# Depthwise convolution by even and odd tokens, conv blocks laid between head pairs, and GpSimd kept for the MLP, in a hybrid RWKV-7 and convolution layer

## The chip, the core and the metric

The kernel runs on one core of a Trainium2 chip. The metric is the time of one execution in device microseconds (us), as the median of several runs. Engines are called PE (TensorE, matrix products), DVE (VectorE), ACT (ScalarE), POOL (GpSimd) and SP (SyncE, which issues transfers). Each runs its own queue of instructions in order; a wait of the first holds up all behind it.

## The reference

One layer of 1024 tokens and 1024 channels, in float32. The input is normalised and projected onto 2816 columns; 1792 go to eight RWKV-7 heads, 1024 to a gated convolution of 512 channels with 31 taps. The results are joined and projected back, and an MLP with a squared ReLU follows.

```python
h = rmsnorm(x, norm_mix_g[l])
p = h @ w_in[l]                                  # 1024 x 2816
p_rwkv = p_rwkv + (token_shift(p_rwkv) - p_rwkv) * shift_mu[l]
y_rwkv = rwkv7_group(p_rwkv, ...)                # 8 heads x 64, state S_t = S_{t-1}(diag(w_t) + a_t b_t^T) + v_t k_t^T
# conformer_conv_group
h = u[..., :D_CONV] * jax.nn.sigmoid(u[..., D_CONV:])
h = lax.conv_general_dilated(h, conv_w[:, None, :], window_strides=(1,),
        padding=[(30, 0)], feature_group_count=512) + conv_b
# ... layer norm over the 512 channels, silu
x = x + jnp.concatenate([y_rwkv, y_conv], axis=-1) @ w_out[l]
h = rmsnorm(x, norm_mlp_g[l])
x = x + jnp.square(jax.nn.relu(h @ w_ff1[l])) @ w_ff2[l]
return rmsnorm(x, norm_final_g)
```

## The kernel before

**Products.** An operand is split into a high and a low part and multiplied in three products (high by high, low by high, high by low). The input projection takes 22 weight blocks of 128 columns: `load_w` fetches a block into `wraw` (one buffer), ACT rounds it to `wh` (L219) and POOL forms `wl`, the rest (L220); there are two buffers of each. A block is multiplied in two halves of 512 tokens, each 48 matmuls of 256 columns (8 slices of channels, three products, two pieces of 256 tokens).

**Convolution.** Channels lie on partitions, in four blocks of 128. `conv_block(cb)` projects a block's two halves (gate and value), writes the gated result `h2` of 30 + 1024 columns (L312), and puts 31 taps into a list: a first one that also adds the bias (L317) and 30 that multiply `h2`, shifted by a token each, by one weight per channel and add it to `acc` (L319), each on all 1024 columns, on DVE. `do_taps(n)` writes out the next n taps.

**RWKV heads.** The heads go in four pairs p of 0 to 3 and two halves of 512 tokens. `decays` makes the decays with a scan (L407); `mix_block` projects r, k and v; `stage1(p, h)` forms what the recurrence needs in chunks of 64 tokens (AR at L425 and L426, kq, KB, AM at L448, a diagonal `dg` at L456 by which KB is multiplied on PE for `kt`); `solve(g)` inverts the triangular systems of a group of two pairs in 30 rounds of two small DVE operations (L505, L507); `merge(g, h)` brings its result through DRAM back to another layout (QT, L524). Then `step(g)` runs one of 16 chunks of a group's recurrence: POOL scales the state (`SP`, L585), PE multiplies, DVE adds the new state (L601).

**After them.** `conv_norm` transposes and normalises the convolution's channels and splits them (`cvl`, L669); `load_wout` splits the output weights (`wol`, L692); `out_first` and `out_second` add output products to the residual (L699), `post` finishes a head group's output (`yo`, L629). The first products of the MLP are mixed in, and the MLP itself follows by half-size blocks.

**Order.** A written-out sequence of calls at the end of the program gives each call its priority; a scheduler places instructions by it and by their dependences, engine by engine. The two lines of `load_w` that split a block are

```python
        S.activation(wh, raw, AF.Copy)
        G.tensor_tensor(wl, raw, wh.bitcast(F32), op=ALU.subtract)
```

where `S` is ACT, `G` POOL and `V` DVE. Every matmul is recorded at L96 and every transpose on PE at L99, inside a helper; there the names of the PSUM banks (ca, cb, ya, yb, ps, pr) tell the work apart.

Of the kernel before, what the change touches and what calls it, by code (L numbers as in the profile page):

```python
# [9 lines left out]
F32 = mybir.dt.float32  # L10
# [21 lines left out]
CUT = (2, 2)  # L32
H2B = 2
DIRECT = 4
# [18 lines left out]
def hymba_layer(ctx: ExitStack, tc: tile.TileContext, a: dict, out: bass.AP):  # L53
# [242 lines left out]

    accs = [None] * 4
    taps = []
    gate = {"solve": None}

    def conv_block(cb):
        tag = in_banks[-1]
        wg, wu = load_w(CG + cb * P), load_w(CU + cb * P)
        h2 = hc.tile([P, TAPS - 1 + T], F32, name="h2", bufs=H2B)
        V.memset(h2[:, 0:TAPS - 1], 0.0)
# [7 lines left out]
        accs[cb] = cv.tile([P, T], F32, name="acc", bufs=4)  # L313

        def tap(j):
            if j == 0:
                return V.tensor_scalar(accs[cb], h2[:, 0:T], cw[:, 0, cb:cb + 1], prm("conv_b", cb), op0=ALU.mult, op1=ALU.add)  # L317
            else:
                return V.scalar_tensor_tensor(accs[cb], h2[:, j:j + T], cw[:, j, cb:cb + 1], accs[cb], op0=ALU.mult, op1=ALU.add)  # L319
# [97 lines left out]
    def stage1(p, h):  # L417
# [22 lines left out]
        G.tensor_tensor(KB[:, :, 1, :], c8(kq), c8(Ei), op=ALU.mult)  # L440
        for i in range(2):
# [133 lines left out]
    def chain(g, c, yb):  # L575
        e = c % 2
        L1, KB, rhs, Arb, Th = tiles.pop((g, c))
        b = bank("ca" if g == 0 else "cb")
        lo = b.t[0:64, 0:256].rearrange("p (n t) -> p n t", n=4)
        hi = b.t[0:64, 256:512].rearrange("p (n t) -> p n t", n=4)  # L580
        yr = yb.t[64 * e:64 * e + 64, 0:256].rearrange("p (n t) -> p n t", n=4)
        SR = cp.tile([P, 4, C], F32, name="SR", bufs=2)
        SP, R = SR[0:C], SR[C:P]
        if c < 15:
            G.tensor_tensor(SP, rhs[0:64], PC[:, c, 4 * g:4 * g + 4, None].to_broadcast([C, 4, C]), op=ALU.mult)  # L585
        hops = []
        for n in range(4):
            i = b.mm(lo[:, n, :], L1[:, n, 0:C], rhs[:, n, :], True, True)
        hops.append(i)
        S.copy(R, lo)  # L590
        for n in range(4):
            yb.mm(yr[:, n, :], L1[:, n, C:P], rhs[:, n, :], n == 0, False)
        for n in range(4):
            i = b.mm(lo[:, n, :], Th[:, n, :], R[:, n, :], True, True)
        hops.append(i)
        S.copy(rhs[0:64], lo)
        if c < 15:
            for n in range(4):
                i = b.mm(hi[:, n, :], KB[:, n, :], rhs[:, n, :], True, True)
            hops.append(i)  # L600
            V.tensor_tensor(tiles[g, c + 1][2][0:64], hi, SP, op=ALU.add)  # L601
        for n in range(4):
            yb.mm(yr[:, n, :], Arb[:, n, :], rhs[0:64, n, :], False, n == 3)
        if g == 1:
            pace.update(hops=hops, n=0)

    def post(pool, d):
# [19 lines left out]
        for p in range(NP):  # L627
            S.activation(yo[:, p, :], b.t[:, p * P:(p + 1) * P], AF.Identity, scale=prm("ln_x_g", p), bias=prm("ln_x_b", p))
        G.tensor_tensor(yo, yo, bon, op=ALU.add)  # L629
        V.tensor_tensor(yo, yo, bg.t.rearrange("p (n t) -> p n t", n=NP), op=ALU.mult)  # L630
# [6 lines left out]
    def conv_norm(ln, ct, h):  # L637
        yc = [ln.tile([P, 512], F32, name=f"yc{t}") for t in range(4)]
        mv = ln.tile([P, 4, 2], F32, name="mv")
        for t in range(4):  # L640
            b = bank()
            for cb in range(4):
                b.tr(b.t[:, cb * P:(cb + 1) * P], accs[cb][:, (4 * h + t) * P:(4 * h + t + 1) * P], ident)
# [13 lines left out]
        for cb in range(4):  # L657
# [26 lines left out]
    def load_wout(pool, raws, ks):  # L684
        for n in range(2):
            for k in ks:
# [288 lines left out]
    stage1(1, 1)  # L975
    do_taps(4)
    do_taps(4)
    do_taps(4)
    do_taps(4)
    do_taps(4)  # L980
    do_taps(4)
    do_taps(4)
    do_taps(4)
    do_taps(4)
    do_taps(4)
    do_taps(4)
    do_taps(4)
    do_taps(2)
# [60 lines left out]
    step(0)  # L1049
    step(0)  # L1050
# [307 lines left out]
```

## Time and profile before

| | us |
|---|---|
| median of 3 runs | 1330.41 |
| lowest and highest run | 1326.93 and 1331.7 |
| the profiled execution, by the same clock as the runs | 1334.43 |
| its span in the trace, first to last instruction | 1332.7 |
| PE busy in it | 1229.8 |
| DVE busy | 960.9 |
| ACT busy | 539.6 |
| POOL busy | 291.1 |

Busy times are sums over instructions, with overlaps counted once. Matmuls overlap in the record, so PE's is no measure of how fast it works. The mean granted clock of PE over the span is .961 of full speed.

### The profile page before, as it was taken

Reading aid. Unit: us, or ns where it says so; the run is one execution under the profiler, and the core shown is the slowest. Engines: PE = TensorE matmul, PEld = TensorE weight load, DVE = VectorE, ACT = ScalarE, POOL = GpSimd, SP = SyncE. Lnnn points to the kernel's source line nnn. Section 1 sums busy time; section 2 is a strip of 40 time slices with the busy share of each in tenths; the row PEclk is TensorE's granted clock in tenths of the full one; section 3 lists DMA queues with packets and bytes.
Section 4 is the critical chain, followed back from the end, with each engine's and each line's share of the span. In section 5 each row is a group of like instructions: output and inputs, shape, how many; then the busy total and the mean of one; then the engine's idle time right before and its main releaser. Section 6 shows DMA issues by size and latency. Waiting matters only on the chain.

```text
span 1332.7 us, 20860 instructions
## 1 busy us (share of the span) xinstructions
PE 1229.8 (92%) x8171; PEld 1059.0 (79%) x8171; DVE 960.9 (72%) x1440; ACT 539.6 (40%) x937; POOL 291.1 (22%) x181
## 2 busy tenths in 40 slices
PE   6999899988998859999999999999948899999996
PEld 5999788887896748899988788888837688888885
DVE  6379965698999672444669766665428898897997
ACT  6313233322323363333468454545533333433345
POOL 2124143332333153311000000000004324231420
PEclk9999899998998778999999999999978899999999
DMA  5211445525626667536135554543157425223003
GB/s 185 56 48 37 109 112 145 132 72 122 155 59 158 160 162 186 176 112 178 44 110 183 159 162 142 163 134 124 66 167 267 142 80 158 63 81 93 16 1 126
DMA packets 194475, 161.44 MB, mean 121 GB/s; under 512 B 54387, under 2 KB 153785, under 8 KB 194377
## 3 DMA queue, kind: packets, MB, share of 16 engines
q1 hardware_dynamic: 181192, 157.90, 40.0%
q10 hardware_dynamic: 13056, 2.13, 0.9%
q8 instruction: 64, 1.05, 0.3%
q14 instruction: 35, 0.28, 0.1%
q0 software_dynamic: 128, 0.08, 0.0%
HBM read 110.23 MB, written 49.84 MB: 120 GB/s over the span
## 4 chain that ended last, share of the span: by engine, by line
PE 60%; DVE 24%; DMA 7%; issue 4%; ACT 2%; SPq 1%; POOL 1%; DVEq 0%; ACTq 0%
PE ps L96 27%; DVE acc L319 9%; PE yb L96 9%; PE ya L96 8%; PE cb L96 7%; PE ca L96 5%; PE pr L96 3%; DMA lk_d<-kt 2%; DVE Q L507 2%; DVE Qt L505 1%; DVE bl L827 1%; DVE sA L1187 1%; DVE al L827 1%; DVE ta L437 1%; PE ps L99 1%
## 5 line engine op out<-in xcount | busy, mean ns | idle before, releaser
L319 DVE SCALAR_TENSOR_TENSOR acc<-h,cw,acc 128x1024 f32<-128x1024 f32 x120 | 176.8, 1493 | 1.1
L826 ACT ACTIVATE ah<-sA 128x1024 fp32r<-128x1024 f32 x32 | 34.0, 1061 | 135.3 <-PE pr L96 50.1
L96 PE MATMUL ps<-bh,ah 128*128 128x512 f32 x168 | 65.7, 404 | 22.4 <-ACT bh L826 16.5
L220 POOL TENSOR_TENSOR wl<-wraw,wh 128x1024 fp32r<-128x1024 f32 x22 | 56.6, 2572 | 136.1 <-ACT wh L219 136.1
L1187 POOL TENSOR_TENSOR sB<-B,B11e 128x1024 f32<-128x1024 f32 x4 | 11.6, 2890 | 337.5 <-DMA B<-in_w_ff_dram 335.2
L96 PE MATMUL cb<-hh,wh 128*128 128x256 f32 x264 | 79.4, 301 | 5.1 <-DVE k L257 3.1
L96 PE MATMUL cb<-hl,wh 128*128 128x256 f32 x264 | 79.9, 302 | 0.1
L96 PE MATMUL cb<-hh,wl 128*128 128x256 f32 x264 | 77.8, 295 | 0.0
L96 PE MATMUL ps<-bl,ah 128*128 128x512 f32 x168 | 68.1, 405 | 4.0 <-DVE bl L827 3.9
L96 PE MATMUL yb<-hh,wl 128*128 128x256 f32 x248 | 71.5, 288 | 0.0
L96 PE MATMUL yb<-hh,wh 128*128 128x256 f32 x248 | 71.4, 288 | 0.0
L96 PE MATMUL yb<-hl,wh 128*128 128x256 f32 x248 | 71.0, 286 | 0.0
L96 PE MATMUL ps<-bh,al 128*128 128x512 f32 x168 | 67.5, 402 | 0.0
L827 DVE TENSOR_TENSOR al<-sA,ah 128x1024 fp32r<-128x1024 f32 x32 | 50.5, 1580 | 23.6 <-ACT ah L826 23.6
L827 DVE TENSOR_TENSOR w1l<-s,w1h 128x512 fp32r<-128x512 f32 x64 | 43.9, 687 | 24.8 <-ACT w1h L826 24.8
L826 ACT ACTIVATE w1h<-s 128x512 fp32r<-128x512 f32 x64 | 40.3, 632 | 50.5 <-PE ps L96 29.0
L96 PEld LDWEIGHTS cb<-hh,wh 128*128 128x128 f32 x264 | 53.2, 202 | 9.0 <-DVE k L257 3.3
L96 PEld LDWEIGHTS cb<-hl,wh 128*128 128x128 f32 x264 | 53.1, 201 | 4.8 <-issue 4.0
L96 PEld LDWEIGHTS ps<-bh,ah 128*128 128x128 f32 x168 | 32.9, 197 | 30.2 <-ACT bh L826 16.9
L585 POOL TENSOR_TENSOR SR<-rhs,PC 64x256 f32<-64x256 f32 x30 | 28.6, 953 | 124.8 <-DVE rhs L601 104.8
L96 PEld LDWEIGHTS cb<-hh,wl 128*128 128x128 f32 x264 | 53.3, 202 | 2.3 <-issue 2.0
L846 ACT ACTIVATE c<-c 128x512 f32<-128x512 f32 x60 | 38.0, 633 | 38.2 <-DVE c L932 21.5
(460 smaller groups left out, 4008.8 us busy)
## 6 DMA issues: line engine op xcount, KB each, us to landing
w1r<-in_w_ff_dram SPq DMA_DIRECT2D x44, 512.0 KB
hid_d<-c SPq DMA_DIRECT2D x64, 256.0 KB
LK<-lk_d SPq DMA_DIRECT2D x32, 384.0 KB
A<-hid_d SPq DMA_DIRECT2D x24, 512.0 KB
B<-in_w_ff_dram SPq DMA_DIRECT2D x24, 512.0 KB
wraw<-in_w_in_dram SPq DMA_DIRECT2D x22, 512.0 KB
xt<-in_x_dram SPq DMA_DIRECT2D x8, 512.0 KB
lk_d<-AR SPq DMA_DIRECT2D x16, 256.0 KB
```

The source lines that it names most:

```text
L96: return self._order(PE.matmul(o, lhsT=lhsT, rhs=rhs, start=start, stop=stop, skip_group_check=more))
L99: self._order(PE.transpose(o, in_, identity))
L220: G.tensor_tensor(wl, raw, wh.bitcast(F32), op=ALU.subtract)
L319: return V.scalar_tensor_tensor(accs[cb], h2[:, j:j + T], cw[:, j, cb:cb + 1], accs[cb], op0=ALU.mult, op1=ALU.add)
L437: V.scalar_tensor_tensor(ta, ta, 1.0, Ei, op0=ALU.add, op1=ALU.mult)
L505: V.tensor_tensor(o, Q[:, 0:s, s:s + 1].to_broadcast([R, s, n]), Q[:, s:s + 1, s + 1:32].to_broadcast([R, s, n]), op=ALU.mult)
L507: V.tensor_tensor(Q[:, 0:s, s + 1:32], Q[:, 0:s, s + 1:32], o, op=ALU.add)
L585: G.tensor_tensor(SP, rhs[0:64], PC[:, c, 4 * g:4 * g + 4, None].to_broadcast([C, 4, C]), op=ALU.mult)
L826: S.activation(hi, src, AF.Copy)
L827: V.tensor_tensor(lo, src, hi.bitcast(F32), op=ALU.subtract)
L846: S.activation(c, c if src is None else src, AF.Relu)
L1187: engine.tensor_tensor(t, x, y, op=op)
```

## The change

Three things are changed together.

First, the convolution works on even and odd tokens. `h2` has three rows of 16 + 512 columns: even tokens, odd tokens and their sums (two sums of 256 columns each at L318 after, behind the two h2 writes at L316). The 16 even taps act on the even tokens (into `acc[:, 0]`), the 15 odd taps on the odd ones (into `odd`), and 16 taps with summed weights (`cws`) on the sums (into `acc[:, 1]`); `join` subtracts the first two from the third for the odd outputs and adds them, one token apart, for the even ones. So 31 operations on 1024 columns become 47 on 512 (three of them first ones, which also add the bias) and 3 joins on 512. `h2` has one buffer where it had two. `conv_norm` reads the halves and writes its results at a stride of two columns.

Second, whatever POOL did ahead of the MLP on large tiles goes to DVE: `wl` (22 times), kq, KB and r in `stage1` (8 each), `SP` (30), `wol` (16), `yo` (8) and `cvl` (8). `dg` and its product are replaced: ACT scales KB by the decay (64 operations of 128x128, into `kd`), and PE transposes that.

Third, the sequence of calls is rewritten: a conv block stands ahead of each head pair, with its taps behind the pair's `stage1`; conv block 3 comes after `stage1(3, 1)`; `solve(1)` and the merges come ahead of `conv_norm`; and steps of group 1 begin between those of group 0.

```diff
-H2B = 2
+H2B = 1
...
-        G.tensor_tensor(wl, raw, wh.bitcast(F32), op=ALU.subtract)
+        V.tensor_tensor(wl, raw, wh.bitcast(F32), op=ALU.subtract)
...
+    cws = const.tile([P, 16, 4], F32, name="cws")
+    V.tensor_copy(cws[:, 0], cw[:, 0])
+    V.tensor_tensor(cws[:, 1:16], cw[:, 1:30:2], cw[:, 2:31:2], op=ALU.add)
+    cb2 = derived("cb2", 4, prm("conv_b", 0, 4), 2.0, None)
...
-        h2 = hc.tile([P, TAPS - 1 + T], F32, name="h2", bufs=H2B)
+        h2 = hc.tile([P, 3, 16 + 512], F32, name="h2", bufs=H2B)
...
-            o = TAPS - 1 + h * 512
-            V.scalar_tensor_tensor(h2[:, o:o + 512], th, 1.0, bu, op0=ALU.add, op1=ALU.mult)
...
+            o = slice(16 + h * 256, 16 + h * 256 + 256)
+            V.scalar_tensor_tensor(h2[:, 0:2, o].rearrange("p e n -> p n e"), th.rearrange("p (n e) -> p n e", e=2), 1.0,
+                                   bu.rearrange("p (n e) -> p n e", e=2), op0=ALU.add, op1=ALU.mult)
+            V.tensor_tensor(h2[:, 2, o], h2[:, 0, o], h2[:, 1, o], op=ALU.add)
...
+            o, c = ((acc[:, 0], cw[:, 2 * i, cb:cb + 1]), (odd[:, 1:513], cw[:, max(2 * i - 1, 0), cb:cb + 1]), (acc[:, 1], cws[:, i, cb:cb + 1]))[ph]
+            x = h2[:, ph, i + 1:i + 1 + 512]
...
+            return V.scalar_tensor_tensor(o, x, c, o, op0=ALU.mult, op1=ALU.add)
...
+        def join(*_):
+            V.tensor_tensor(acc[:, 1], acc[:, 1], acc[:, 0], op=ALU.subtract)
+            V.tensor_tensor(acc[:, 1], acc[:, 1], odd[:, 1:513], op=ALU.subtract)
+            return V.tensor_tensor(acc[:, 0], acc[:, 0], odd[:, 0:512], op=ALU.add)
...
-        G.tensor_tensor(kq, kq, k, op=ALU.mult)
+        V.tensor_tensor(kq, kq, k, op=ALU.mult)
...
-            dg = mp.tile([P, 4, P], F32, name="dg", bufs=1)
-            G.tensor_tensor(dg, ident[:, None, :].to_broadcast([P, 4, P]),
-                            E1[:, 4 * q:4 * q + 4, C:C + 1].to_broadcast([P, 4, P]), op=ALU.mult)
+            kd = mp.tile([P, 4, P], F32, name="kd", bufs=1)
+            for c in range(4):
+                S.activation(kd[:, c, :], KB[:, 4 * q + c].rearrange("p j t -> p (j t)"), AF.Copy, scale=E1[:, 4 * q + c, C:C + 1])
...
-                bk.mm(bk.t[:, c * P:(c + 1) * P], KB[:, 4 * q + c].rearrange("p j t -> p (j t)"), dg[:, c, :], True, True)
+                bk.tr(bk.t[:, c * P:(c + 1) * P], kd[:, c, :], ident)
...
-            G.tensor_tensor(SP, rhs[0:64], PC[:, c, 4 * g:4 * g + 4, None].to_broadcast([C, 4, C]), op=ALU.mult)
+            V.tensor_tensor(SP, rhs[0:64], PC[:, c, 4 * g:4 * g + 4, None].to_broadcast([C, 4, C]), op=ALU.mult)
...
+    step(0)
+    conv_block(3)
     do_taps(8)
-    stage1(3, 1)
-    step(0)
-    step(0)
+    step(0)
+    solve(1, (0, 1))
+    step(0)
+    merge(1, 0)
+    step(0)
+    do_taps(23)
...
-    solve(1, (0, 1))
+    step(0)
     wo = open_pool("wo", side="right")
     load_wout(wo, wo, (4, 5, 6, 7))
-    merge(1, 0)
-    step(0)
-    merge(1, 1)
-    step(0)
-    step(0)
-    step(0)
+    step(0)
+    step(1)
+    step(0)
+    step(1)
```

On DVE, in the first `stage1` of head pair 0, the queue of before alternates taps of the two conv blocks (h_719 is block 0's h2, h_936 block 1's):

```order
L319 SCALAR_TENSOR_TENSOR acc<-h_936,cw,acc 128x1024
L437 SCALAR_TENSOR_TENSOR ta<-ta,Ei 128x512
L319 SCALAR_TENSOR_TENSOR acc<-h_719,cw,acc 128x1024
L337 MEMSET pm 128x1
L425 SCALAR_TENSOR_TENSOR AR<-k,nkk,E_1151 128x8x64
L319 SCALAR_TENSOR_TENSOR acc<-h_936,cw,acc 128x1024
L439 SCALAR_TENSOR_TENSOR KB<-k,par_104,ta 128x8x64
L319 SCALAR_TENSOR_TENSOR acc<-h_719,cw,acc 128x1024
```

In the changed kernel the same place on DVE reads (h_724 is block 0's h2; L460, L448 and L462 are the old L437, L425 and L439):

```order
L460 SCALAR_TENSOR_TENSOR ta<-ta,Ei 128x512
L331 SCALAR_TENSOR_TENSOR odd<-h_724,cw,odd 128x512
L257 SCALAR_TENSOR_TENSOR k<-yb,omu,pm 128x512
L331 SCALAR_TENSOR_TENSOR acc<-h_724,cws,acc 128x512
L331 SCALAR_TENSOR_TENSOR acc<-h_724,cw,acc 128x512
L331 SCALAR_TENSOR_TENSOR odd<-h_724,cw,odd 128x512
L360 MEMSET pm 128x1
L448 SCALAR_TENSOR_TENSOR AR<-k,nkk,E_942 128x8x64
L459 TENSOR_TENSOR kq<-kq,k 128x512
L462 SCALAR_TENSOR_TENSOR KB<-k,par_104,ta 128x8x64
L331 SCALAR_TENSOR_TENSOR acc<-h_724,cws,acc 128x512
L331 SCALAR_TENSOR_TENSOR acc<-h_724,cw,acc 128x512
```

Block 1's taps are no longer there; half taps of block 0, in three accumulations, stand between the head's operations, and kq of POOL has moved in.

On DVE, at the end of `solve(1)`, the queue of before goes straight on to `conv_norm` (L665), the merge's transposes (L524) and output products (L699):

```order
L507 TENSOR_TENSOR Q<-Q,Qt 128x30
L509 TENSOR_TENSOR Q<-Q,nup 128x1024
L665 SCALAR_TENSOR_TENSOR hn<-th_5107,hn 128x512
L665 SCALAR_TENSOR_TENSOR hn<-th_5121,hn 128x512
L524 STREAM_TRANSPOSE QT<-QS 128x256
L665 SCALAR_TENSOR_TENSOR hn<-th_5135,hn 128x512
L665 SCALAR_TENSOR_TENSOR hn<-th_5149,hn 128x512
L699 TENSOR_TENSOR x_0_4448<-xr,ps 128x512
```

In the changed kernel the same place on DVE reads (h_4194 is block 3's h2; L532 is the old L509, L624 the rhs add, L608 SP):

```order
L530 TENSOR_TENSOR Q<-Q,Qt 128x30
L532 TENSOR_TENSOR Q<-Q,nup 128x1024
L331 SCALAR_TENSOR_TENSOR acc<-h_4194,cw,acc 128x512
L330 TENSOR_SCALAR acc<-h_4194,cws,cb_667 128x512
L328 TENSOR_SCALAR odd<-h_4194,cw 128x512
L624 TENSOR_TENSOR rhs<-ca,SR 64x256
L608 TENSOR_TENSOR SR<-rhs,PC 64x256
L331 SCALAR_TENSOR_TENSOR acc<-h_4194,cw,acc 128x512
L331 SCALAR_TENSOR_TENSOR acc<-h_4194,cws,acc 128x512
L331 SCALAR_TENSOR_TENSOR odd<-h_4194,cw,odd 128x512
```

The taps of block 3 have moved behind the solve, with rhs adds and SP of group 0's steps between them; the two transposes of the merge (now L547) follow among them, and `conv_norm` and the output products come after the join.

## Rows read from the trace of the kernel before

**Rows 1.** The page: busy time of each engine; the last chain by engine.

```profile
PE 1229.8 (92%) x8171; PEld 1059.0 (79%) x8171; DVE 960.9 (72%) x1440; ACT 539.6 (40%) x937; POOL 291.1 (22%) x181
PE 60%; DVE 24%; DMA 7%; issue 4%; ACT 2%; SPq 1%; POOL 1%; DVEq 0%; ACTq 0%
```

**Rows 2.** Stages: length, busy PE, PEld, DVE, ACT, POOL, granted clock, DMA share, GB/s.

```profile
0.00:74.00 74.00, 61.81 (x456) 58.56 (x457) 33.44 (x121) 35.22 (x70) 16.70 (x22) 1.00 0.36 114
74.00:147.00 73.00, 69.70 (x542) 67.06 (x540) 72.50 (x57) 17.41 (x30) 22.71 (x10) 0.95 0.19 54
147.00:255.00 108.00, 99.75 (x696) 86.86 (x696) 67.42 (x69) 33.41 (x60) 37.52 (x26) 0.95 0.51 128
255.00:293.00 38.00, 33.65 (x265) 31.83 (x264) 36.09 (x77) 11.75 (x23) 10.76 (x6) 1.00 0.29 77
293.00:424.00 131.00, 122.35 (x1239) 105.04 (x1237) 124.80 (x118) 36.62 (x74) 39.53 (x25) 0.97 0.49 118
424.00:451.00 27.00, 22.89 (x154) 18.74 (x155) 16.99 (x20) 7.08 (x16) 9.29 (x7) 0.62 0.60 148
451.00:490.00 39.00, 29.06 (x303) 23.48 (x302) 37.30 (x113) 24.77 (x47) 14.05 (x13) 0.88 0.62 173
490.00:510.00 20.00, 11.64 (x175) 9.56 (x174) 4.81 (x7) 11.86 (x22) 11.23 (x9) 0.64 0.62 144
510.00:738.00 228.00, 224.53 (x1953) 202.96 (x1953) 130.98 (x321) 107.10 (x240) 31.03 (x31) 1.00 0.49 146
```

**Rows 3.** Chain and PE's timeline: start, us, then the piece with its count.

```profile
67.81 5.78 PE ya L96 x48
676.60 2.72 PE ca L96 x12
189.77 1.05 PE L96 MATMUL ps<-dg,KB 128*128 128x128 f32 x8
```

**Rows 4.** DVE by line, 0 to 700 us: count, busy us, mean ns, idle before.

```profile
L319 DVE SCALAR_TENSOR_TENSOR acc<-h,cw,acc 128x1024 f32<-128x1024 f32 x120 | 176.8, 1493 | 1.1
L437 DVE SCALAR_TENSOR_TENSOR ta<-ta,Ei 128x512 f32<-128x512 f32 x8 | 14.5, 1810 | 0.0
L425 DVE SCALAR_TENSOR_TENSOR AR<-k,nkk,E 128x512 f32<-128x512 f32 x8 | 14.3, 1787 | 2.0 <-ACT E L411 1.6 <-issue 0.3
L317 DVE TENSOR_SCALAR acc<-h,cw,par 128x1024 f32<-128x1024 f32 x4 | 5.6, 1403 | 0.0
```

**Rows 5.** Timeline of DVE and of POOL around 100 us: start, us.

```profile
100.15 2.90 DVE L317 TENSOR_SCALAR acc<-h,cw,par 128x1024 f32<-128x1024 f32 x1
104.50 2.47 DVE L319 SCALAR_TENSOR_TENSOR acc<-h,cw,acc 128x1024 f32<-128x1024 f32 x2
99.87 2.63 POOL L220 TENSOR_TENSOR wl<-wraw,wh 128x1024 fp32r<-128x1024 f32 x1 [5.15 <-ACT wh L219]
```

**Rows 6.** DVE by line, 0 to 700 us, operations that stand away from POOL's.

```profile
L827 DVE TENSOR_TENSOR w1l<-w1r,w1h 128x512 fp32r<-128x512 f32 x12 | 8.2, 687 | 2.1 <-ACT w1h L826 1.0 <-PE ya L96 0.5 <-PE yb L96 0.5
L509 DVE TENSOR_TENSOR Q<-Q,nup 128x1024 f32<-128x1024 f32 x2 | 2.5, 1225 | 0.1
L601 DVE TENSOR_TENSOR rhs<-ca,SR 64x256 f32<-64x256 f32 x15 | 6.2, 411 | 0.6 <-PE ca L96 0.6
```

**Rows 7.** POOL by line, 0 to 738 us: count, busy us, mean ns, idle before.

```profile
L220 POOL TENSOR_TENSOR wl<-wraw,wh 128x1024 fp32r<-128x1024 f32 x22 | 56.6, 2572 | 136.1 <-ACT wh L219 136.1
L585 POOL TENSOR_TENSOR SR<-rhs,PC 64x256 f32<-64x256 f32 x30 | 28.6, 953 | 124.8 <-DVE rhs L601 104.8 <-DVE nt L123 10.5 <-DVE mv L647 5.1
```

**Rows 8.** ACT by line, 74 to 738 us: the scaling of 128x128 in post.

```profile
L628 ACT ACTIVATE yo<-ca,par 128x128 f32<-128x128 f32 x32 | 12.1, 458 | 12.7 <-PE ca L99 12.7
```

**Rows 9.** DVE's timeline, the first QT of merge(1): start, us, idle before.

```profile
496.79 0.45 DVE L524 STREAM_TRANSPOSE QT<-QS 128x256 f32<-128x256 f32 x1 [2.91 <-DMA QS<-qd_d]
```

**Rows 10.** Users of the tile wraw: who waited, idle us, times.

```profile
  POOL wl L220: 136.1, 17
  ACT wh L219: 21.9, 7
```

More of the change, by code (lines that the diff above doesn't have):

```diff
@@ L310, in conv_block @@
             bu = in_proj(wu, h * 512, 512, tag)
-            o = TAPS - 1 + h * 512
-            V.scalar_tensor_tensor(h2[:, o:o + 512], th, 1.0, bu, op0=ALU.add, op1=ALU.mult)
[L313 to L319, printed above, removed]
@@ L321, in conv_block @@
-        taps.extend((tap, j) for j in range(TAPS))
+            o = slice(16 + h * 256, 16 + h * 256 + 256)
+            V.scalar_tensor_tensor(h2[:, 0:2, o].rearrange("p e n -> p n e"), th.rearrange("p (n e) -> p n e", e=2), 1.0,
+                                   bu.rearrange("p (n e) -> p n e", e=2), op0=ALU.add, op1=ALU.mult)
+            V.tensor_tensor(h2[:, 2, o], h2[:, 0, o], h2[:, 1, o], op=ALU.add)
+        acc = accs[cb] = cv.tile([P, 2, 512], F32, name="acc", bufs=4)
+        odd = mp.tile([P, 513], F32, name="odd", bufs=1)
@@ new lines, in tap @@
+        def tap(ph, i):
+            o, c = ((acc[:, 0], cw[:, 2 * i, cb:cb + 1]), (odd[:, 1:513], cw[:, max(2 * i - 1, 0), cb:cb + 1]), (acc[:, 1], cws[:, i, cb:cb + 1]))[ph]
+            x = h2[:, ph, i + 1:i + 1 + 512]
+            if ph == 1 and i == 1:
+                V.memset(odd[:, 0:1], 0.0)
+                return V.tensor_scalar(o, x, c, None, op0=ALU.mult)
+            if i == 0:
+                return V.tensor_scalar(o, x, c, prm("conv_b", cb) if ph == 0 else cb2[:, cb:cb + 1], op0=ALU.mult, op1=ALU.add)
+            return V.scalar_tensor_tensor(o, x, c, o, op0=ALU.mult, op1=ALU.add)
@@ L323, in do_taps @@
+        def join(*_):
+            V.tensor_tensor(acc[:, 1], acc[:, 1], acc[:, 0], op=ALU.subtract)
+            V.tensor_tensor(acc[:, 1], acc[:, 1], odd[:, 1:513], op=ALU.subtract)
+            return V.tensor_tensor(acc[:, 0], acc[:, 0], odd[:, 0:512], op=ALU.add)
+        taps.extend((tap, (ph, i)) for ph in (0, 2, 1) for i in range(ph == 1, 16))
+        taps.append((join, ()))
+    tapped = [0, 0]
     def do_taps(n):
-        for f, j in taps[:n]:
-            i = f(j)
+        tapped[0] += n
+        for f, j in taps[:tapped[0] * 48 // TAPS - tapped[1]]:
+            i = f(*j)
@@ L326, in do_taps @@
             if gate["solve"] is not None:
                 tc.add_manual_dep(i.ins, gate["solve"].ins.name, NOSYNC, reason="solve first")
+        n = tapped[0] * 48 // TAPS - tapped[1]
+        tapped[1] += n
         del taps[:n]
@@ L628, in post @@
             S.activation(yo[:, p, :], b.t[:, p * P:(p + 1) * P], AF.Identity, scale=prm("ln_x_g", p), bias=prm("ln_x_b", p))
-        G.tensor_tensor(yo, yo, bon, op=ALU.add)
+        V.tensor_tensor(yo, yo, bon, op=ALU.add)
         V.tensor_tensor(yo, yo, bg.t.rearrange("p (n t) -> p n t", n=NP), op=ALU.mult)
@@ L642, in conv_norm @@
             for cb in range(4):
[L643 removed]
+                n0 = 256 * h + 128 * (t % 2)
+                b.tr(b.t[:, cb * P:(cb + 1) * P], accs[cb][:, t // 2, n0:n0 + 128], ident)
             st = small.tile([P, 6], F32, name="st")
@@ L667, in conv_norm @@
             cl = ct.tile([P, 512], F32R, name=f"cvl{cb}", bufs=2)
-            S.activation(ch, hn, AF.Copy)
-            G.tensor_tensor(cl, hn, ch.bitcast(F32), op=ALU.subtract)
+            hv = hn.rearrange("p (e n) -> p e n", e=2)
+            S.activation(ch.rearrange("p (n e) -> p e n", e=2), hv, AF.Copy)
+            V.tensor_tensor(cl.rearrange("p (n e) -> p e n", e=2), hv, ch.bitcast(F32).rearrange("p (n e) -> p e n", e=2), op=ALU.subtract)
             res.append((ch, cl))
@@ L691, in load_wout @@
                 S.activation(wh, raw, AF.Copy)
-                G.tensor_tensor(wl, raw, wh.bitcast(F32), op=ALU.subtract)
+                V.tensor_tensor(wl, raw, wh.bitcast(F32), op=ALU.subtract)
                 wos[k, n] = wh, wl
@@ L967, in hymba_layer @@
     stage1(0, 1)
+    do_taps(31)
+    conv_block(1)
     decays(1, 0)
     mix_block(5, (0, 1))
-    do_taps(4)
     mix_block(1, (0, 1))
@@ L975, in hymba_layer @@
     stage1(1, 1)
[L976 to L988, printed above, removed]
+    do_taps(31)
+    conv_block(2)
     solve(0, (0, 1))
@@ L1027, in hymba_layer @@
     mix_block(3, (0, 1))
+    step(0)
     mix_block(11, (0, 1))
+    do_taps(15)
+    step(0)
     stage1(3, 0)
     decays(3, 1)
-    do_taps(8)
+    step(0)
     stage1(3, 1)
     step(0)
+    conv_block(3)
+    do_taps(8)
     step(0)
+    solve(1, (0, 1))
[3 more added lines that the diff above has]
+    do_taps(23)
+    assert not taps
+    step(0)
+    merge(1, 1)
     step(0)
     done_in()
+    cycles["any"] = ("ps", "ps", "ps", "pr")
     ct = open_pool("ct", side="right")
@@ L1062, in hymba_layer @@
     step(0)
+    assert steps[0] == 16
+    cycles["any"] = ("ps", "ca", "ps", "ya", "ps", "pr")
     out_first(wo, 0, 0)
-    step(1)
-    step(1)
     step(1)
@@ L1130, in hymba_layer @@
     close_pool("nx")
+    assert steps[1] == 16
     ph2.close()
+    cycles["any"] = ("ps", "ca", "ya", "ps", "cb", "pr", "ps", "yb")
     fpb = open_pool("fpb", side="right")
```

31 lines of the change are left out of this document (4 added, 27 removed).

## The prediction

> **What bounds the kernel now.** Read first the page's busy shares and its chain of what ended last [rows 1]: TensorE (PE) is busy 92% of the span, yet only 60% of the chain is PE's; 24% is VectorE's (DVE), which is busy 72%. An average cannot say where a change pays, so read next the busy time by stage [rows 2]. From 738 us to the end the MLP runs, which the change does not touch. Ahead of it there are three regimes. From 74 to 147, 255 to 293, 293 to 424 and 451 to 490 us DVE is busy 72.50, 36.09, 124.80 and 37.30 us, 270.7 of 281: DVE is the bound. From 147 to 255 PE is busy 99.75 of 108. From 424 to 451 and from 490 to 510 neither is full, DVE at 16.99 of 27 and 4.81 of 20, and the granted clock is .62 and .64. From 510 to 738 PE is the bound, 224.53 of 228.
>
> PE's busy time flatters it, since matmul records overlap. The chain gives its pace: 48 matmuls of 256 columns in 5.78 us, .120 each, and 12 of 512 in 2.72, .227 each; a small product of 128 columns takes .131 [rows 3]. Matmuls counted by form at such paces need some 54 us in the first 74, some 336 of the 436 from 74 to 510, and some 208 in the 228 after. So the whole loss is about 20 + 100 + 20 us, and the middle stretch is what the change rearranges.
>
> DVE there works slowly as well as much. A tap of 128x1024 takes 1493 ns on the mean of 120 and the first tap of a block 1403 [rows 4], but two run back to back in 2.47 us, so 1.24 each [rows 5]. The reason stands beside them: the first tap that started at 100.15 took 2.90 us while GpSimd (POOL) split a weight block from 99.87 for 2.63 [rows 5]. The other operations on two SBUF tiles stretch likewise: 1810 and 1787 ns for 512 columns of L437 and L425 [rows 4], against 687 where POOL is quiet [rows 6]. Over all such operations before the MLP, the mean less the shortest row of the same form comes to about 73 us: 33 in the taps (120 x .25, and 4 firsts), 40 elsewhere, of which 9.0 is L437 (8 x 1.12) and 8.8 L425.
>
> **The change, part by part.**
>
> *Taps.* Before, 176.8 + 5.6 us [rows 4]. After, a block takes 47 operations and 3 joins on 512 columns at .687 [rows 6], 34.4 us, and two sums of 256 at an estimated .36 (half of .687 and a little): 35.1, four times 140; the three first ones, like L317 with one SBUF operand, should be shorter, which makes 137. Saved 45, of which 33 is POOL's disturbance and only 12 the arithmetic. A half tap costs no less than half of 1.24, .62, and by the rows no more than .69: 124 to 140 in all. The h2 writes now go out at a stride of two, and so do the low parts of the conv output: no row shows that; 16 operations at .69 to twice .69, 0 to 11 us extra, which I take up with the waits below.
>
> *POOL's work to DVE.* 22 wl at 1.225 (a 128x1024 operation of two tensors), 27.0; 24 kq, KB and r, 16 wol, 8 yo and 8 cvl at .687, 38.5; 30 SP at the .411 of the rhs add [rows 6], 12.3: 77.8 us more. POOL took 2572 ns for a wl and 953 for an SP [rows 7], so each dependent also gets its operand sooner. With POOL silent the other 40 us of disturbance go. Net for DVE before the MLP: -45 - 40 + 78 = -7. The sum therefore turns on where the work stands, not on its amount.
>
> *dg.* 64 products of two passes become 64 transposes of one: at .131 a pass [rows 3], -8.4 us of PE. In their place ACT scales 64 tiles of 128x128, .458 each by L628, which has a bias as well [rows 8]; bounds .2 and .46 us, 13 to 29 in all. ACT is busy 143 of the 436 us [rows 2], so this hides; uncovered, two batches of four stand in each of the 8 head halves ahead of a transpose, some 1.8 us each.
>
> *Order.* I counted both engines' instructions between the marks of the new order, each at its price above. From the second h2 write to the first output product, DVE against PE: taps of block 0 51.9/52.8; to block 1's h2 12.1/21.4; its taps 52.3/55.3; to the solve 16.1/23.5; solve(0) 38.2/39; to the join of block 2 47.3/36.7; to the last h2 write 39.7/72; rest of solve(1) 25.6/11; the remaining taps of block 3 28.6/10; to the first output product 32.6/30. DVE sums to 344 (before 360, of 436), the larger of each pair to 398. The same reckoning for before (270.7 of DVE in its four stretches, 91 of PE in the second, 17 and 6 in the two thin ones) gives 384, so 52 us stood above it. Of these, 24 were the two thin stretches: in the second DVE waited for the merge's trip through DRAM (2.91 us at 496.79 [rows 9]) with no tap left ahead of it. After the change solve(1) ends with some 33 half taps still queued, 22 us, which cover the trip. I keep the remaining 28, and add 4 for waits on wl (bounds 0 and 45, third rival) and for the strided writes together: 398 + 32 = 430, **6 less** than 436. Bounds 408 (a fifth of the loss of before) and 448 (all of it).
>
> In the 228 us after, PE is full, so what is moved ahead of them is worth its length: 22 rather than 15 rhs adds stand before the first output product, so 7 chain steps of some 2.3 us of PE leave it, 16 us; counted through, PE has 191 us there for 208. With the same 20 of loss: **17 less**. The first 74 us: wl now waits in DVE's queue inside the first norm's short operations, so the start moves 0 to 2 us later; I take **+1**. H2B 2 to 1 gives up the second h2 tile: block 1's h2 write waits for block 0's last tap, but in the new order the join stands ahead of that write on DVE anyway, so PE can wait but DVE doesn't. I take nothing, and the 9 us by which PE exceeds DVE there are in the 398.
>
> Sum, on the profiled execution: 1334.4 - 6 - 17 + 1 = 1312.4. It ran 4.0 above the median of 1330.4, so 1308.5, say **1309**. With the middle kept within 14 of its 430, some two thirds of the way to either bound, its own range is 1294 to 1323.
>
> **A rule against the change.** The stretch from the last h2 write to the first output product holds 87 us of DVE work (25.6 + 28.6 + 32.6) and 51 of PE. The three rows from 424 to 510, as thin, ran at granted clocks of .62, .88 and .64, so now at 2.4 and now at 1.2 GHz, .74 on the mean over their lengths [rows 2]; at that PE's 51 become 69 and still lie under 87. The Trainium skill ("TensorE: Matmul & The Clock Gate", Part 1: The HAM clock gate) says that the throttled clock is the default and that activity releases it. By that alone the whole stretch would run at 1.2 GHz, PE's part would be 102 and the sum 15 higher; the rows at .62 to .88 agree with the direction but not with the whole of it.
>
> **Rivals.**
>
> *Nearly no waits (better).* The remaining 28 of before came from DVE operations stretched by POOL and from PE waiting behind them. With POOL silent, the middle falls to 408 and the next stage to 208: 22 + 3 more than forecast, 1284. For it: in its four stretches DVE idled only 10 of 281 us, so what makes it lighter there is time won. Against it: at each of the ten marks one engine waits for the other, and each hand-over can cost.
>
> *The loss only moves (no change).* PE runs the thin tail at 1.2 GHz throughout, twice 51 for DVE's 87 and so +15, or the seven steps moved ahead are lost again in the tail, +17, since their rhs adds and SP stand between taps in DVE's queue; 1324 to 1327, a gain of about 4. For it: the clock was low wherever PE was thin [rows 2]. Decided by whether PE is the last to finish in that tail.
>
> *DVE waits for the weights (slower).* wl stands in DVE's in-order queue and needs wh of ACT, which needs the raw tile: one buffer only. Before, POOL waited for ACT's wh 17 times, 136.1 us, 8 on the mean, and ACT for the transfer 7 times, 21.9 [rows 10]; on POOL that cost nothing. On DVE all that is queued behind, taps and AM evictions and rhs adds, waits too. 18 of the 22 wl stand in the middle stretch, 11 or 12 where DVE is the bound; at 2.5 us each it is +30: 1338 to 1340. The point from which it decides is 22 us of such waits, 2 a wl. Against it: the raw tile is free as soon as wl is done, 1.2 us after wh where POOL took 2.6.
>
> **How the numbers follow.** Forecast .52, nearly no waits .15, loss moved .17, waits for weights .16. The range 1282 to 1337 takes in the first three and the lower part of the last. A difference under 0.5%, 6.7 us, can't be told from none: faster is below 1323.8 (.52 + .15), the third case is the same, the last slower.
>
> **What would show it.** In the changed profile: taps of 512 columns at .62 to .69 with no long ones; wl on DVE at 1.2; POOL idle from 20 to 738 us; L471 to L495 near .69. DVE busy about 344 us in the stretch from the second h2 write to the first output product, 430 long; the QT transposes without a DMA wait of 2 us or more; the next stretch 211 long. Wrong if DVE sits idle before wl for more than 22 us (third rival), if the strided writes take 1.4, if PE's granted clock is near .5 through the tail and PE ends it, or if ACT's scaling shows as PE's wait.

## The result

The changed kernel takes 1310.95 us in the median of 4 runs (1310.67 to 1311.71), the kernel before beside it 1331.03 (4 runs). The ratio is 0.9856, with a 95% interval of 0.9836 to 0.9877: faster by 1.4%. Side by side on another chip it was 0.9841 (0.9818 to 0.9863). The forecast was 1309, in a range of 1282 to 1337, with a chance of .67 for faster. The profiled execution took 1310.69 us, its span is 1309.0, 23.7 less than before.

**The page after.** Busy time of each engine, and the last chain by engine, which answer to [rows 1]:

```profile
PE 1223.2 (93%) x8107; PEld 1058.3 (81%) x8107; DVE 943.7 (72%) x1639; ACT 559.1 (43%) x1001; POOL 100.6 (8%) x57
PE 65%; DVE 7%; DMA 3%; ACT 2%; issue 1%; SPq 0%; ACTq 0%; DVEq 0%
```

DVE's busy time fell by 17 us only, but its part of the chain from 24% to 7%. Its load is nearly the same; it sets the end much less.

**Stages after**, cut at the marks by which the prediction counted (second h2 write, joins, begin and end of the solves, last h2 write, first output product, last early product); columns as in [rows 2]:

```profile
75.00:129.00 54.00, 54.00 (x432) 51.35 (x429) 50.74 (x80) 18.30 (x37) 0.11 (x1) 1.00 0.29 78
129.00:152.00 23.00, 23.00 (x163) 19.46 (x162) 12.95 (x21) 11.36 (x23) 0.11 (x1) 1.00 0.45 111
152.00:205.00 53.00, 53.00 (x411) 49.11 (x410) 50.44 (x80) 18.18 (x37) 0.12 (x1) 1.00 0.36 95
205.00:238.00 33.00, 32.90 (x235) 27.69 (x234) 16.33 (x25) 12.30 (x25) 0.11 (x1) 1.00 0.82 196
238.00:278.00 40.00, 39.79 (x317) 37.29 (x316) 36.44 (x90) 16.48 (x35) 0.11 (x1) 1.00 0.28 72
278.00:326.00 48.00, 43.95 (x507) 36.56 (x506) 45.70 (x75) 18.26 (x40) 0.11 (x1) 0.86 0.66 155
326.00:399.00 73.00, 73.00 (x663) 64.59 (x662) 38.94 (x79) 27.41 (x63) 0.11 (x1) 1.00 0.56 143
399.00:424.00 25.00, 19.90 (x205) 17.14 (x203) 23.84 (x62) 4.39 (x12) 0.00 (x0) 0.72 0.44 122
424.00:452.00 28.00, 19.55 (x337) 17.41 (x340) 27.23 (x47) 4.05 (x12) 0.30 (x1) 0.56 0.58 128
452.00:511.00 59.00, 49.61 (x483) 42.51 (x483) 30.32 (x80) 37.42 (x70) 0.00 (x0) 0.72 0.54 152
511.00:713.00 202.00, 200.52 (x1535) 182.07 (x1533) 135.12 (x336) 100.35 (x220) 0.00 (x0) 1.00 0.46 139
```

Compare these lengths with the larger of each pair in the prediction: 52.8 forecast and 54 measured, 21.4 and 23, 55.3 and 53, 23.5 and 33, 39 and 40, 47.3 and 48, 72 and 73, 25.6 and 25, 28.6 and 28, 32.6 and 59. Eight of ten are within 2.5 us. The whole excess stands in two places. Some 10 us stand ahead of solve(0), where TensorE is busy 32.90 of 33: at the prediction's paces the 235 matmuls of that stretch come to some 30 us for the 23.5 counted, an estimate, and some 4 of the difference had been counted for the stretch before it. The other 26 us stand between the last join and the first output product, where neither engine is full on the average (DVE 30.32 of 59, PE 49.61). PE's is more than the 30 us counted; its granted clock changes there. Two pieces of that stretch:

```profile
452.00:457.00 5.00, 5.00 (x96) 4.52 (x96) 0.91 (x3) 1.11 (x3) 0.00 (x0) 0.50 0.35 97
462.00:467.00 5.00, 4.26 (x74) 3.83 (x72) 2.52 (x11) 2.42 (x6) 0.00 (x0) 1.00 0.42 98
```

In the first, at half the full clock, PE is busy throughout; in the second, at the full clock, it has gaps. At the mean clock of .72 the 30 us would be some 42, so by this estimate the clock accounts for 12 of the 26 us at most; no run shows its part.

**VectorE by line**, 0 to 700 us, which answers to [rows 4, 6]; then ACT's scaling, for [rows 8]:

```profile
L331 DVE SCALAR_TENSOR_TENSOR acc<-h,cw,acc 128x512 f32<-128x512 f32 x60 | 44.5, 742 | 0.0
L220 DVE TENSOR_TENSOR wl<-wraw,wh 128x1024 fp32r<-128x1024 f32 x22 | 26.8, 1220 | 19.6 <-ACT wh L219 19.5
L608 DVE TENSOR_TENSOR SR<-rhs,PC 64x256 f32<-64x256 f32 x30 | 12.3, 413 | 0.6 <-POOL rhs L592 0.2
L460 DVE SCALAR_TENSOR_TENSOR ta<-ta,Ei 128x512 f32<-128x512 f32 x8 | 5.5, 684 | 0.5 <-ACT kq L458 0.5
L448 DVE SCALAR_TENSOR_TENSOR AR<-k,nkk,E 128x512 f32<-128x512 f32 x8 | 6.0, 745 | 1.9 <-ACT E L434 1.1 <-issue 0.8
```

```profile
L480 ACT ACTIVATE kd<-KB,E 128x128 f32<-128x128 f32 x64 | 20.5, 392 | 3.8 <-DVE KB L463 2.8 <-DVE KB L462 1.0
```

L460 is the old L437, 684 ns for 1810; L448 the old L425, 745 for 1787. The disturbance is gone. The moved operations cost what was forecast (1220 and 413 ns for 1225 and 411, kd .392 between .2 and .46). A half tap takes 742 ns, not the .687 that I used, and DVE did wait for wh, 19.5 us.

### The profile page after: what moved, and what is told of

It is laid out like the page before. It is cut to its first block, busy times and chain, and to the rows that moved or that the text cites. A ratio compares the mean times of both kernels' runs of the same rounds, so it can differ in the third digit from the quotient of the medians.

```text
span 1309.0 us, 20808 instructions
## 1 busy us (share of the span) xinstructions
PE 1223.2 (93%) x8107; PEld 1058.3 (81%) x8107; DVE 943.7 (72%) x1639; ACT 559.1 (43%) x1001; POOL 100.6 (8%) x57
## 4 chain that ended last, share of the span: by engine, by line
PE 65%; DVE 7%; DMA 3%; ACT 2%; issue 1%; SPq 0%; ACTq 0%; DVEq 0%
PE ps L96 29%; PE yb L96 10%; PE ya L96 8%; PE cb L96 8%; PE ca L96 6%; PE pr L96 4%; DVE al L852 1%; PE ps L99 1%; DVE acc L331 1%; DVE sA L1189 1%; DMA woraw<-in_w_out_dram 1%; DVE x L1220 1%; DMA hid_d<-c 1%; DVE bl L852 1%; DVE odd L331 0%
## 5 line engine op out<-in xcount | busy, mean ns | idle before, releaser
L96 PE MATMUL cb<-hh,wh 128*128 128x256 f32 x248 | 72.7, 293 | 1.5 <-ACT hh L243 1.5
L96 PE MATMUL cb<-hl,wh 128*128 128x256 f32 x248 | 72.9, 294 | 0.3 <-DVE hl L244 0.3
L852 DVE TENSOR_TENSOR al<-sA,ah 128x1024 fp32r<-128x1024 f32 x32 | 55.0, 1718 | 23.5 <-ACT ah L851 23.5
L96 PE MATMUL cb<-hh,wl 128*128 128x256 f32 x248 | 71.7, 289 | 0.0
L96 PE MATMUL yb<-hh,wl 128*128 128x256 f32 x232 | 66.6, 287 | 0.0
L96 PEld LDWEIGHTS cb<-hh,wh 128*128 128x128 f32 x248 | 48.3, 195 | 5.4 <-ACT hh L243 1.9
L96 PEld LDWEIGHTS cb<-hl,wh 128*128 128x128 f32 x248 | 48.3, 195 | 4.8 <-issue 4.0
L96 PEld LDWEIGHTS cb<-hh,wl 128*128 128x128 f32 x248 | 48.1, 194 | 2.3 <-issue 2.1
L851 ACT ACTIVATE w1h<-w1r 128x512 fp32r<-128x512 f32 x48 | 30.2, 631 | 42.5 <-PE ps L96 26.6
L852 DVE TENSOR_TENSOR w1l<-w1r,w1h 128x512 fp32r<-128x512 f32 x48 | 33.0, 689 | 19.7 <-ACT w1h L851 19.7
L96 PEld LDWEIGHTS yb<-hh,wh 128*128 128x128 f32 x232 | 44.6, 192 | 3.1 <-issue 2.1
```

What stands on the lines that cost most here:

```text
L96: return self._order(PE.matmul(o, lhsT=lhsT, rhs=rhs, start=start, stop=stop, skip_group_check=more))
L851: S.activation(hi, src, AF.Copy)
L852: V.tensor_tensor(lo, src, hi.bitcast(F32), op=ALU.subtract)
```

## The experiments

All are compared with the kernel before, run on the same chip.

**Which part of the change pays?** First the changed kernel with the convolution of before:

```diff
-        h2 = hc.tile([P, 3, 16 + 512], F32, name="h2", bufs=H2B)
+        h2 = hc.tile([P, TAPS - 1 + T], F32, name="h2", bufs=H2B)
...
-        taps.extend((tap, (ph, i)) for ph in (0, 2, 1) for i in range(ph == 1, 16))
-        taps.append((join, ()))
+        taps.extend((tap, j) for j in range(TAPS))
```

> The changed kernel with the convolution of before: 31 taps on 1024 columns, h2 and the accumulators in token order; POOL still silent, order of calls unchanged. In the changed kernel the convolution costs DVE 131.0 us of half taps (745 ns each), some 5 of first ones, 8 of joins, 3.4 of sums and 2.9 more for strided h2 writes, about 150.5; 31 undisturbed full taps (1.24 and .81) cost 152. Theory (the halving buys DVE nothing, the gain is the order's and the moves'): 1308 to 1314 us, full taps at 1.24 to 1.27. Rival (the halving is worth the 12 us that the prediction gave it): 1318 to 1323.

Measured 1317.43 us, 0.9886 (0.9852 to 0.9919) of before, beside other runs of the kernel before than the changed kernel's. The interval reaches into that of the changed kernel, so both were run again on one chip:

> The changed kernel itself, on the same chip as the next, so that the two can be set side by side: 0.984 to 0.988 of before.

> The changed kernel with the convolution of before, again, beside the changed kernel itself. Its DVE had 153.2 us of full taps at 1277 ns and 3 of first ones, where the changed kernel has some 150.5. Theory (the halving is worth what DVE saves where it is the bound, 6 us): 3 to 8 us above the changed kernel. Rival (nothing): within 2. Rival (the prediction's 12): 10 or more above.

The changed kernel 1312.03, 0.9841 (0.9818 to 0.9863); with full taps 1317.09, 0.9878 (0.986 to 0.9897). The difference is 5.1 us, and no run of the one falls among the runs of the other (1310.59 to 1314.99 and 1316.24 to 1318.61). The full taps in the second:

```profile
L319 DVE SCALAR_TENSOR_TENSOR acc<-h,cw,acc 128x1024 f32<-128x1024 f32 x120 | 153.2, 1277 | 1.6
```

With four first ones at .81 that is 156.4 us. The halved convolution costs 131.0 (176 half taps) + 6.3 (firsts) + 8.2 (joins) + 3.4 (sums) + 3.0 (h2 writes that take 1055 ns on the mean for 686), 151.9. The 4.5 us between them agree with the 5.1 measured: halving the convolution is worth 5 us, more than the nothing of the first theory and less than the 12 of the prediction.

Then the sequence of calls alone (convolution, POOL's operations and the diagonal product as before), and the same with the new convolution:

```diff
-        V.tensor_tensor(wl, raw, wh.bitcast(F32), op=ALU.subtract)
+        G.tensor_tensor(wl, raw, wh.bitcast(F32), op=ALU.subtract)
...
-            V.tensor_tensor(SP, rhs[0:64], PC[:, c, 4 * g:4 * g + 4, None].to_broadcast([C, 4, C]), op=ALU.mult)
+            G.tensor_tensor(SP, rhs[0:64], PC[:, c, 4 * g:4 * g + 4, None].to_broadcast([C, 4, C]), op=ALU.mult)
```

> The changed kernel with the convolution of before and with all of POOL's operations and the diagonal product back on POOL: what is left of the change is the sequence of calls and the single h2 buffer. Theory (in sum the moves cost DVE 78 us and give back 73, so they hardly matter, and the order is the gain): 1311 to 1320. Rival (a silent POOL is the gain): within 4 of 1331. A third (order and moves need each other, since POOL's longer wl and SP now stand ahead of work that nothing covers): slower than 1331.

> The changed kernel with all of POOL's operations and the diagonal product back on POOL; convolution by even and odd tokens and order as changed. Half taps are stretched by POOL's work as full ones were, so by the theory it stands like the order alone, 1312 to 1322, with half taps near .9 on the mean. If a silent POOL is the gain: 1325 to 1335.

Measured 1353.24, 1.0162 (1.0124 to 1.02), and 1351.72, 1.0147 (1.0113 to 1.0182). The theory that the order is the gain falls, and the third one, that the order needs the moves, is borne out: by itself the order makes the kernel 21 us **slower**. "The order" here is the sequence of calls with the single h2 buffer and a new rotation of the PSUM banks (`cycles`) that came with it; these were not parted. In the order alone the full taps take 1494 ns on the mean, as before, and with the new convolution the half taps 844 to 899. And the moves alone, in the old order with the old convolution:

> The kernel before with only POOL's work moved to DVE and the diagonal product replaced by scaling on ACT; convolution and order of calls as before. DVE gets 78 us of work and loses some 73 of disturbance. Theory: no change, 1325 to 1335, and the full taps at 1.24 to 1.27. Rival (a silent POOL is the gain): 1311 to 1316. Rival (DVE is the bound and the work counts, since the disturbance was hidden): 1360 to 1380.

Measured 1337.25, 1.0037 (1.0019 to 1.0056): no gain, and 5 us lost. Neither half does anything good, and together (full_taps) they give 15 to 16 us. Two questions follow: why a silent POOL gains nothing in the old order, and why POOL costs so much in the new one.

**Why the moves alone gain nothing.** Up to the last h2 write they do gain. Before, then with the moves alone, from the second h2 write to the last:

```profile
74.00:357.00 283.00, 261.85 (x2162) 234.66 (x2161) 234.72 (x256) 79.52 (x145) 87.15 (x53) 0.96 0.40 101
```

```profile
73.00:330.00 257.00, 247.58 (x2079) 221.74 (x2078) 204.17 (x285) 95.77 (x197) 0.69 (x6) 0.97 0.44 113
```

The stretch is 26 us shorter and DVE has 30.5 us less in it, although it does POOL's work: of the moved operations only wl, most of stage1's and two SP stand here. Nine taps, 11.5 of the 30.5 us, have only moved behind that mark (73 full taps in the stretch for 82), but solve(1) too begins 26 us earlier, with 3 taps left over. Of this gain nothing is left at the eighth output product, which ends at 558.0 for 556.9. In between wol, the split of the output weights, now sits in DVE's queue. Users of the tile woraw in that kernel, with who waited, idle us and times:

```profile
L692 DVE TENSOR_TENSOR wol<-woraw,woh x16: 676/693/694, 473.9 to 541.5; 128x512 fp32r<-128x512 f32 x16
...
  ACT woh L691: 15.0, 8
...
  ACT woh L691: 24.6, 11
```

The second line is DVE waiting for woh, 15.0 us in 8 times; the third ACT waiting for the transfers. Taking wol back to POOL, and only that, tests it:

```diff
-                V.tensor_tensor(wl, raw, wh.bitcast(F32), op=ALU.subtract)
+                G.tensor_tensor(wl, raw, wh.bitcast(F32), op=ALU.subtract)
                 wos[k, n] = wh, wl
```

> The kernel before with POOL's work moved to DVE, but the 16 splits of the output weights (wol) left on POOL. With all of it moved, the last h2 write came 27 us earlier than before (330 for 357) and the solve of group 1 began 26 earlier, but the solve took 56 us for 38, with DVE waiting 15.0 us for woh ahead of wol, and the first 8 output products were no earlier than before. Theory (wol in DVE's queue holds up the solve): solve(1) in 38 to 45 us, 1315 to 1325. Rival (what is lost is the chain of group 1 and the output weights' transfers, wherever wol is made): 1328 to 1338.

Measured 1315.88, 0.9873 (0.9843 to 0.9903). So 16 short operations in the wrong queue cost the old order 21 us, as much as the whole change gains, and the old order with the old convolution comes within 4 us of the changed kernel; its interval overlaps that one's, so these runs do not tell the two apart. My place for it was only partly right: the solve still takes 52 us (56 with wol on DVE, 38 before), and ends 5 us sooner. The eighth output product ends 12 us sooner, at 545.6, and the last one 16 us sooner, at 676.9. The chain of the moves alone, 483 to 560 us, is 26.5% woraw transfers, four of them from 517 to 541 one behind the other:

```profile
517.08 6.24 DMA woraw<-in_w_out_dram
523.34 0.64 ACT woh L691
524.00 0.70 DVE wol L692
524.72 2.85 DMA woraw<-in_w_out_dram
527.57 0.69 DVE wol L692
```

A raw tile (there are two) comes free when wol has read it, and wol waits its turn in DVE's queue, so the next transfer starts late. With wol on POOL the chain of 478 to 560 has 15.9% of woraw, and the waits for woh (22.0 us there) stand in POOL's queue, where no taps, rhs adds or evictions stand behind them. Why the solve itself is longer with POOL silent stays open: its DVE idles some 15 of 57 us, among others behind rhs adds that wait for PE at a granted clock of .6.

**Why POOL costs so much in the new order.** In the changed kernel one group of its operations at a time was put back: wl; SP; kq, KB, r and the diagonal product of stage1.

```diff
-            V.tensor_tensor(SP, rhs[0:64], PC[:, c, 4 * g:4 * g + 4, None].to_broadcast([C, 4, C]), op=ALU.mult)
+            G.tensor_tensor(SP, rhs[0:64], PC[:, c, 4 * g:4 * g + 4, None].to_broadcast([C, 4, C]), op=ALU.mult)
...
-        V.tensor_tensor(kq, kq, k, op=ALU.mult)
+        G.tensor_tensor(kq, kq, k, op=ALU.mult)
...
-                bk.tr(bk.t[:, c * P:(c + 1) * P], kd[:, c, :], ident)
+                bk.mm(bk.t[:, c * P:(c + 1) * P], KB[:, 4 * q + c].rearrange("p j t -> p (j t)"), dg[:, c, :], True, True)
```

> The changed kernel with only the 22 splits of the input weights (wl) back on POOL: 57 us of POOL for 27 us of DVE. With all of POOL's work back the new order costs 41 us more than the changed kernel. Theory A (POOL's work costs by disturbing DVE, in proportion to POOL's busy time, 57 of 193 us): 1320 to 1327. Theory B (it costs where a slower result stands ahead of work that waits for it; wl is made ahead of need): 1305 to 1313, and DVE's waits for wh vanish.

> The changed kernel with only the 30 state scalings SP back on POOL, .95 us for .41, 29 us of POOL. Theory A (disturbance, 29 of 193 us of POOL): 1315 to 1320. Theory B (waiting results; SP is used only after three hops of the chain step, so it has slack): 1308 to 1313.

> The changed kernel with kq, KB, r and the diagonal product of stage1 back on POOL (62 us of POOL, 16 of DVE and 64 products of two passes for transposes of one). Theory A (disturbance, 62 of 193 us): 1322 to 1330 with the 8 us of PE. Theory B (kq and KB stand between k and the products of AM, 1.7 us each for .69, twice in each of 8 head halves, and the diagonal ahead of kt): 1330 to 1342.

Measured 1327.0 (0.9955; 0.9929 to 0.9982), 1317.22 (0.9876; 0.9831 to 0.9921) and 1328.4 (0.9967; 0.9946 to 0.9989). By its ratio the changed kernel would stand at 1312.3 on this chip, so wl costs 15 us and the stage1 group 16. The 5 us of SP can't be told from nothing, since its interval takes in the whole of the changed kernel's (0.9836 to 0.9877). POOL's operations take 60.5, 38.1 and 61.2 us in these runs. All three times lie in theory A's ranges, but its cause shows only in two of them. The half taps with wl on POOL (up to 411 us), then with SP on POOL:

```profile
L331 DVE SCALAR_TENSOR_TENSOR acc<-h,cw,acc 128x512 f32<-128x512 f32 x45 | 39.0, 867 | 0.0
L331 DVE SCALAR_TENSOR_TENSOR acc<-h,cw,acc 128x512 f32<-128x512 f32 x60 | 44.5, 742 | 0.0
```

With the stage1 group they take 788 to 812 ns. With SP no half tap takes longer than 751 ns; there it is POOL that waits, with SP operations of up to 5.24 us for a median of .61. In the stage1 group, later results and the 8 us of PE are not parted from the disturbance. The place can be seen with wl. The stretch from the second h2 write to the third, in the changed kernel and then with wl on POOL:

```profile
75.70:132.60 56.90, 56.90 (x446) 53.62 (x447) 51.53 (x83) 19.10 (x39) 0.11 (x1) 1.00 0.31 83
```

```profile
77.00:139.80 62.80, 59.73 (x451) 55.62 (x452) 56.97 (x81) 21.70 (x43) 10.54 (x5) 0.97 0.30 77
```

DVE has less to do there, and is busy 5.4 us longer: 10.54 us of POOL stretch its operations by more than the wl it was spared. PE has no gap in this stretch of the changed kernel (56.90 of 56.90), and DVE idles 5.4 us. With wl on POOL DVE idles as long (5.8), so its longer work has found no slack: the stretch is 5.9 longer, and PE has a gap of 3.1 us, in which it waits for an AM eviction of DVE. The Trainium skill ("GPSIMD Engine Reference", 8. Key points) says that GpSimd shares its SBUF interfaces with VectorE and contends with its instructions on two SBUF inputs; the trace agrees for wl, with half taps at 867 ns (45 of them) for 743, and shows no longer taps for SP.

**Can the rest be had?** The 26 us ahead of the first output product. The chain of the changed kernel, 485 to 505 us, has two transfers of output weights:

```profile
485.47 4.55 DMA woraw<-in_w_out_dram
498.07 3.59 DMA woraw<-in_w_out_dram
```

So the weights were fetched ahead of the first conv_norm, beginning with the half of columns that is used first, and then three output products were set ahead of the second as well:

```diff
-        for n in range(2):
+        for n in ((1, 0) if 7 in ks else (0, 1)):
...
     done_in()
...
+    wo = open_pool("wo", side="right")
+    load_wout(wo, wo, (4, 5, 6, 7))
     sc = open_pool("sc", side="right")
     cTs[0] = conv_norm(sc, ct, 0)
     close_pool("sc")
     step(0)
-    wo = open_pool("wo", side="right")
-    load_wout(wo, wo, (4, 5, 6, 7))
...
+    out_first(wo, 2, 1)
     step(0)
     step(1)
+    out_first(wo, 0, 1)
     step(0)
+    out_first(wo, 1, 1)
     sc = open_pool("sc", side="right")
...
-    out_first(wo, 2, 1)
...
-    out_first(wo, 0, 1)
...
-    out_first(wo, 1, 1)
```

> The changed kernel with the output weights of the convolution channels fetched ahead of the first conv_norm rather than behind it, the half of columns that the first output product takes first. From the last join to the first output product the changed kernel takes 58.9 us for 32.6 of DVE and 30 of PE, and the chain there waits twice for these transfers (4.55 and 3.59 us). Theory (the transfers end that stretch): first output product at about 500 instead of 510, 1301 to 1307. Rival (chain steps and conv_norm end it, or TensorE-bound work after it takes the gain back): 1309 to 1313.

> The changed kernel with the output weights fetched ahead of the first conv_norm and with three output products put ahead of the second conv_norm, where TensorE is thin (30 us of work in 58.9). Fetching alone gave nothing: the first output product ended 3 us earlier and the rest 3 later. Theory (products fill TensorE's idle time in that stretch): first output product near 490, 1302 to 1308. Rival (chain steps end that stretch, and each product set among them delays them): 1309 to 1315.

Measured 1313.11 (0.9861; 0.9807 to 0.9915) and 1314.37 (0.9856; 0.9836 to 0.9877), no better than the changed kernel (1312.03 beside the second). In the first of them the first output product ended at 507.3 for 511.0, and the last early product 3 us later than in the changed kernel, 716.6 for 713.4. So fetching earlier won 4 of the 26 us, although the chain of its 455 to 505 us still has 15.8% of such transfers. In the second the first output product did end near 490, at 491.9, as the theory had it, and nothing was gained: the eighth ended at 549.5 for 544.4, and the last early product at 718.4. The chain of its 495 to 550 us is 25.5% woraw transfers, of the weights that come after. What ends the stretch in the changed kernel stays open: its chain there has chain steps, conv_norm and transfers, none above 14%. No version beat the changed kernel. One was not run: the changed kernel with wol left on POOL, the step that gave the old order 21 us. In the changed kernel DVE waited 4.5 us for woh, for 15.0 in the old order, so less may be had there.

## Why the prediction was right, and where not

*The time.* 1309 for 1311, but out of terms that were off both ways; that the two errors nearly cancel is luck. Start: +1 forecast, +1.3 measured (second h2 write ends at 75.7 for 74.4). Middle: -6 forecast, -1 measured (435.3 for 435.9). The stage after: -17 forecast, -26 measured (202.4 for 228.3). MLP: 0 and +1.5.

*The middle, mis-sized by 5.* The larger of each pair sum to 398 and the stretch took 435. The step was "I keep the remaining 28, and add 4": 37 stood above the sum. It was not spread over hand-overs, as I had taken it; 26 of it stands in the last stretch. DVE was busy 333 us from the second h2 write to the first output product, where 344 were forecast.

*The stage after, mis-sized by 9.* The step was "with the same 20 of loss": PE's work there, at the prediction's paces, comes to some 190 us, an estimate, for the 191 counted, so the loss was some 12. The seven chain steps did leave the stage: 336 matmuls of 64 columns stand in it for 616 before. The middle took them on and is no longer than before.

*Taps.* "47 operations and 3 joins at .687" was wrong by the price: a tap multiplies by one weight per channel and takes 742, where the operation that I priced it by has no such operand. Saved 30.5 of 182.4 us rather than 45, and of these 26 were POOL's disturbance.

*"The sum therefore turns on where the work stands, not on its amount."* The sentence holds, but I applied it to the order and not to the moves. The net of -45 - 40 + 78 hides that the disturbance stood in the main ahead of the last h2 write, where DVE is the bound, and much of the moved work (wol, yo, cvl, most SP) stands behind it, where for the most part it isn't. In the old order too solve(1) begins 26 us earlier for that. The step "what is moved ahead of them is worth its length" remains unproved: no run moved the chain steps alone, and the version without the new order but with wol on POOL is within 4 us.

*The rivals.* The third, DVE waiting for weights, was named for wl. There it happened and cost little: of 19.5 us, 12.0 stand ahead of 75 us and 6.5 in the stretch from 326 to 399, where PE is busy throughout. The same mechanism decided the matter for wol, in the old order. I had priced wol at .687 and given its wait no thought, though the trace of before showed POOL waiting for those weights. The second rival, a slow clock: from 399 to 511 the granted clock was .72, .56 and .72. In the first two DVE was nearly full (23.84 of 25 and 27.23 of 28) and they are as long as counted, so the clock cost nothing there beyond what was counted. In the third this rival came true in part: PE ran at half the full clock in pieces of it, worth at most 12 us by the estimate above. The clock was not low throughout, as the rule by itself would have it. Whether the seven steps moved ahead have a part in these 26 us isn't shown.

*dg.* Right: kd took 20.5 us of ACT, and waited for KB 3.8 us in all.

*Sums.* Two are slightly off, without effect: the whole loss of before gives 398 + 52 = 450 for the upper bound, not 448, and 17 us lost again gives 1326, not 1327.

## What to carry to other kernels

When work moves from one engine to another, sum it by stage, not over the kernel: here DVE's lighter load where it is the bound brought solve(1) 26 us forward, while the net over the kernel was near nothing. Load added elsewhere is not free for that. Look at each moved instruction for what it waits for: in the new engine's queue that wait holds up everything behind it, and 16 operations of .69 us cost 21 us here. Test the parts of a compound change one by one and together, since here each of two was a loss alone (21 and 5 us) and they gained 15 us together.

## What the runs showed that was not expected

- A 128x512 operation with one scalar per channel takes 742 to 745 ns, one with a constant 684 (L331 and L448 against L460). A half tap is .58 of a full one at 1277.
- The h2 write that alternates between two rows of the tile takes 1055 ns on the mean for 686; cvl, written at a stride of two columns, takes 687, as one without. The Trainium skill ("SBUF — State Buffer", Door 1: The DMA port swizzle) says that accesses are free of penalty while at least two in a row fall into the same 16 bytes; both numbers agree with it.
